# Decoder trunk on one core: held-back column sums, a rounded part taken from PSUM, and two first blocks by token half in layer 1

## The chip, the core and the metric

The kernel runs on one core of a Trainium2 chip. The core has TensorE (PE: matmuls and transposes), VectorE (DVE), ScalarE (ACT), GpSimd (POOL) and SyncE (SP), which here issues the loads. Each engine works its own instructions in the order in which the program lists them and waits at an instruction until the semaphores that it names have come. Matmuls write to PSUM, which has eight banks; VectorE and ScalarE carry results from there to SBUF. The metric is the time of one execution on the device in microseconds (us).

## The reference

A two-layer decoder trunk on 256 tokens of width 2048, all in float32. Per layer, with `mod` a row of 6 x 2048 values that depends on the vector `c` alone:

```python
mod = cond @ w_ada[l] + b_ada[l]
shift1, scale1, gate1, shift2, scale2, gate2 = split(mod, 6)
h = rms_norm(x, norm1_w[l]) * (1.0 + scale1) + shift1
mixed = mixer_groups(h, ..., w_in[l], ...)      # four head groups: GLA, retention, sliding window, HGRN2
x = x + gate1 * (mixed @ w_out[l])
h = rms_norm(x, norm2_w[l]) * (1.0 + scale2) + shift2
g_ff, u_ff = split(h @ w_ffn_in[l], 2)
x = x + gate2 * ((silu(g_ff) * u_ff) @ w_ffn_down[l])
```

After both layers comes a last `rms_norm`.

## The kernel before

**Matmuls.** Float32 products are made from three passes of a rounded format. An operand `raw` is split into a rounded part `hi` and a rest `lo = raw - hi`, and a product is `hi*hi + hi*lo + lo*hi`: three matmuls. A weight block is 512 rows by 512 columns. It comes as two *pieces* of 256 rows, 512 KB each. `prepare()` makes one piece: a load into `raw` on SP's queue (nine buffers), ScalarE rounds it (`whi`, line 243), VectorE subtracts (`wlo`, line 246). There are four buffers each of `whi` and `wlo`. `plan` is the list of blocks in the order in which they are used. `fill(n)` prepares pieces until n of them stand ready, and wherever `fill` is called, ScalarE and VectorE get the two splits at that place of their queues.

**Blocks.** `block()` (lines 339 to 341) takes both halves of the 256 tokens for each row tile. `blocks_by_token()` (lines 355 to 357) takes one or two whole blocks for the first 128 tokens (t = 0) and then for the other 128 (t = 1): 12 matmuls for each block and half, six for each piece. It first takes all its pieces, then runs, and after a named place (t, block, row tile) it calls what its table `after` has for it.

**Changes of stage.** Three times the whole residual `x` is needed at once: from the mixer of layer 0 to its FFN (A, near 547 us in the profile), from the FFN of layer 0 to layer 1 (B, near 1299 us), and from the mixer to the FFN of layer 1 (C, near 1756 us). At each, `last_blocks()` runs the last two blocks by token half and, as a half ends, does `add_x` (VectorE: `tmp` = product times gate, `x` = x + tmp; ScalarE: a square with its sum, called `junk`), and then `norm_first`: VectorE adds the four sums (`rstd`), ScalarE takes a root, VectorE inverts it and scales the first 512 columns (`xs`). `norm_steps()` then makes the next activations: TensorE transposes `xs` into a PSUM tile `m`, ScalarE applies scale `a` and shift `s` of each column (four instructions of 128 x 128 into `h`), VectorE rounds `h` (`hTh`) and subtracts (`hTl`). The first group of 512 columns (c = 0) is made by token half, groups 1 to 3 for all tokens at once. The first blocks of the next stage run by token half too, so that t = 0 can start while t = 1 is still being normalised.

**Column sums.** `s` and `a` come from `mod`. `ada()` adds up `cond[k] * w_ada[k]` on VectorE in the background (line 403, paced by `pump()` with due times `dl`), and `reduce_` (line 432) sums the 128 partitions of the result with eight matmuls of one column. `later` holds the reductions for a few blocks and then lets them go; `require(key)` forces one.

Of the kernel before, what the change touches and what calls it, by code (L numbers as in the profile page):

```python
# [11 lines left out]
F32 = mybir.dt.float32  # L12
# [68 lines left out]
def decoder(ctx: ExitStack, tc: tile.TileContext, x_d, c_d, pos_d, w_ada, b_ada, n1_d, w_in, w2_d, b2_d,  # L81
# [196 lines left out]
    done = set()  # L278

    def require(*key):  # L280
        while key not in done:
            if later:
                later.pop(0)[2]()
            else:
                bg.popleft()[1]()
# [131 lines left out]
    def ada_pair(l, which, g, dl, defer=6):  # L417
        base = 0 if which == 1 else 6144
        sv, av = colv[l, "s%d" % which], colv[l, "a%d" % which]
        r = ROWS["n1" if which == 1 else "n2"] + 16 * l  # L420

        def fin(acc):
            if defer:
                later.append([3, ("c", l, which, g), lambda: reduce_(acc)])
            else:
                reduce_(acc)

        def reduce_(a):
            ps = MB([P, 2, 4])
# [64 lines left out]
    def norm_steps(av, sv, his, los, xs, by_token=True):  # L494
        if by_token:
# [4 lines left out]
            for t in range(NT):  # L500
# [4 lines left out]
                for k in range(4):  # L505
                    A.activation(h[:, k], ps[:, k], AF.Identity, scale=av[:, k:k + 1], bias=sv[:, k:k + 1])
                split(h, hi[:, :, t * P:(t + 1) * P], lo[:, :, t * P:(t + 1) * P])
# [510 lines left out]
    for l in range(L):  # L1018
# [4 lines left out]
        else:  # L1023
            for g in range(4):
                for c0 in HG:
                    plan_block(w_in[l], g * 512, c0, 512)
            for c0, w in FIRST[3:]:
                for g in range(4):
# [45 lines left out]
    def hgrn(act, nsteps, l):  # L1074
# [5 lines left out]
        ev_q, ev_f, ev_k = tail_hg(l, pq, pf, qT, Pf, kT)  # L1080
        for g in range(4):
# [5 lines left out]
            if g < 3:  # L1087
                require("c", l, 1, g + 1)
                next(nsteps)
# [14 lines left out]
        chunk(act, W, 5904, 512, pg)  # L1104
        gs = T4([P, NT, 512], n="hg")
        gate_evac(pg, gs, l, 1, 0, 512)
# [126 lines left out]
    def last_blocks(bs, adds, key, nsteps, xs):  # L1233
        def added(t, b):
# [9 lines left out]
            if b == len(bs) - 1:  # L1244
# [3 lines left out]
                else:  # L1248
                    if t:
                        fill()  # L1250
                    xs.append(norm_first(t))

        after = {(t, b): lambda t=t, b=b: added(t, b) for t in range(NT) for b in range(len(bs))}
        if nsteps is not None:
            def first():
                next(nsteps)
                fill()
            after[1, 1, 1] = first
# [11 lines left out]
    for l in range(L):  # L1270
# [50 lines left out]
        for f0, npc in PIECES:  # L1321
            ah, al = [], []
            for c in range(f0, f0 + npc):
# [10 lines left out]
                if c == 0:  # L1334
                    def next_group(l=l):
                        require("c", l, 2, 1)
                        next(nsteps)
# [91 lines left out]
```

## Time and profile before

| | us |
|---|---|
| median of three runs (2508.48 to 2510.01) | 2508.67 |
| the profiled execution's own time | 2509.56 |
| its span, first to last instruction | 2507.8 |
| PE busy | 2408.2 (96%) |
| DVE busy | 1803.0 (72%) |
| ACT busy | 1100.7 (44%) |

The row of PE busy is the one to read first: TensorE is the engine that works nearly all the time, and the other engines and the loads have room. The mean granted clock of TensorE is 0.99. Busy shares are means over stages; what a change at a stage's end is worth has to be read there.

### The profile page before, as it was taken

What the parts mean: (1) busy time and instruction counts of PE and PEld (TensorE: products, weight loads), DVE (VectorE), ACT (ScalarE), POOL (GpSimd) and SP (SyncE); (2) the same over time, 40 slices, a digit from 0 to 9 for tenths busy, and PEclk for the clock granted to TensorE, in tenths of its full rate; (3) what the DMA queues carried; (4) which work ended last, traced back from release to release, by engine and by line L of the source; (5) the groups of instructions that cost most, each with busy time, mean ns of one, the idle gap of its engine ahead of it and who ended that gap; (6) DMA issues with size and microseconds to landing.
All of it is one profiled execution on the core that took longest, in us unless ns stands there. A gap on an engine that the chain in (4) does not pass through costs nothing. (4 is left out here: it accounts for less than half of the span.)

```text
span 2507.8 us, 32376 instructions
## 1 busy us (share of the span) xinstructions
PE 2408.2 (96%) x12030; PEld 2034.0 (81%) x12030; DVE 1803.0 (72%) x2032; ACT 1100.7 (44%) x1476; POOL 133.9 (5%) x143
## 2 busy tenths in 40 slices
PE   3998899999999999999989999999999999999998
PEld 3887778778888888888879998887788888888886
DVE  7898899877777667777767787866777555455456
ACT  3434434444443344344444444554544444443444
POOL 1001221000000000000000122100000000000000
PEclk9999999999999999999999999999999999999999
DMA  9997679968888888788767776666688565555563
GB/s 324 359 338 278 211 242 318 320 235 284 296 283 289 280 271 280 273 274 291 266 213 254 234 227 208 219 225 245 229 288 288 189 194 187 181 199 193 191 202 109
DMA packets 314910, 626.17 MB, mean 250 GB/s; under 512 B 21236, under 2 KB 34400, under 8 KB 314496
## 3 DMA queue, kind: packets, MB, share of 16 engines
q1 hardware_dynamic: 312800, 622.68, 73.4%
q8 instruction: 94, 1.54, 0.2%
q10 hardware_dynamic: 528, 1.14, 0.1%
q0 software_dynamic: 1424, 0.29, 0.1%
q14 instruction: 64, 0.52, 0.1%
HBM read 621.93 MB, written 2.10 MB: 249 GB/s over the span
## 5 line engine op out<-in xcount | busy, mean ns | idle before, releaser
L246 DVE TENSOR_TENSOR wlo<-raw,whi 128x1024 fp32r<-128x1024 f32 (+2 forms) x816 | 970.7, 1197 | 547.9 <-ACT whi L243 526.8
L243 ACT ACTIVATE whi<-raw 128x1024 fp32r<-128x1024 f32 (+2 forms) x816 | 836.5, 1034 | 877.0 <-PE d L341 710.3
L339 PE MATMUL d<-whi,hTh 128*128 128x512 f32 (+2 forms) x1888 | 734.7, 389 | 0.7 <-ACT whi L243 0.6
L340 PE MATMUL d<-wlo,hTh 128*128 128x512 f32 (+2 forms) x1888 | 723.1, 383 | 1.0 <-DVE wlo L246 1.0
L341 PE MATMUL d<-whi,hTl 128*128 128x512 f32 (+2 forms) x1888 | 723.8, 383 | 0.0
L403 DVE SCALAR_TENSOR_TENSOR acc<-raw,cond,acc 128x1024 f32<-128x1024 f32 x384 | 500.5, 1304 | 13.1 <-POOL acc L393 7.3
L341 PEld LDWEIGHTS d<-whi,hTl 128*128 128x128 f32 x1888 | 355.3, 188 | 70.4
L340 PEld LDWEIGHTS d<-wlo,hTh 128*128 128x128 f32 x1888 | 355.9, 189 | 67.9 <-DVE wlo L246 1.6
L339 PEld LDWEIGHTS d<-whi,hTh 128*128 128x128 f32 x1888 | 356.0, 189 | 67.4 <-ACT whi L243 1.3
L339 PE MATMUL d<-whi,ah 128*128 128x512 f32 x672 | 262.7, 391 | 0.0
L341 PE MATMUL d<-whi,al 128*128 128x512 f32 x672 | 261.7, 389 | 0.0
L340 PE MATMUL d<-wlo,ah 128*128 128x512 f32 x672 | 261.5, 389 | 0.0
L341 PEld LDWEIGHTS d<-whi,al 128*128 128x128 f32 x672 | 126.2, 188 | 26.5
L340 PEld LDWEIGHTS d<-wlo,ah 128*128 128x128 f32 x672 | 126.2, 188 | 25.9
L339 PEld LDWEIGHTS d<-whi,ah 128*128 128x128 f32 x672 | 126.2, 188 | 25.7
L376 PE MATMUL d<-hTh,whi 128*128 128x256 f32 x320 | 93.1, 291 | 4.6 <-DVE hTh L245 4.6
L339 PE MATMUL d<-whi,mh 128*128 128x512 f32 x224 | 89.5, 400 | 3.8 <-DVE tmp L999 3.4
L378 PE MATMUL d<-hTl,whi 128*128 128x256 f32 x320 | 92.4, 289 | 0.7 <-DVE hTl L246 0.7
L377 PE MATMUL d<-hTh,wlo 128*128 128x256 f32 x320 | 92.0, 288 | 0.0
L340 PE MATMUL d<-wlo,mh 128*128 128x512 f32 x224 | 88.2, 394 | 2.5 <-DVE wlo L246 2.5
L341 PE MATMUL d<-whi,ml 128*128 128x512 f32 x224 | 87.8, 392 | 0.0
L339 PE MATMUL m<-whi,hTh 128*128 128x512 f32 (+2 forms) x184 | 68.5, 372 | 6.3 <-DVE hg L1127 4.7
(286 smaller groups left out, 2161.0 us busy)
## 6 DMA issues: line engine op xcount, KB each, us to landing
raw<-in_w_ada_dram SPq DMA_DIRECT2D x384, 512.0 KB, 5.3
raw<-in_w_ffn_in_dram SPq DMA_DIRECT2D x352, 512.0 KB, 4.7
raw<-in_w_in_dram SPq DMA_DIRECT2D x176, 512.0 KB, 5.3
raw<-in_w_ffn_down_dram SPq DMA_DIRECT2D x176, 512.0 KB, 4.8
raw<-in_w_out_dram SPq DMA_DIRECT2D x64, 512.0 KB, 5.3
raw<-in_w_in_dram SPq DMA_DIRECT2D x32, 256.0 KB, 3.3
raw<-in_w_in_dram SPq DMA_DIRECT2D x16, 272.0 KB, 3.7
x<-in_x_dram SPq DMA_DIRECT2D x2, 1024.0 KB, 9.1
```

The costliest lines, as they stand in the source:

```text
L243: A.activation(hi, src, AF.Copy)
L246: V.tensor_tensor(out=lo, in0=src, in1=hi.bitcast(F32), op=ALU.subtract)
L339: TE.matmul(o, xh, wh[:, kk], start=st, stop=False)
L340: TE.matmul(o, xh, wl[:, kk], start=False, stop=False)
L341: TE.matmul(o, xl, wh[:, kk], start=False, stop=sp)
L376: TE.matmul(o, a, hi4[:, k], start=st and f % 2 == 0, stop=False, skip_group_check=True)
L377: TE.matmul(o, b, hi4[:, k], start=False, stop=False, skip_group_check=True)
L378: TE.matmul(o, a, lo4[:, k], start=False, stop=sp and f % 2 == 1, skip_group_check=True)
L403: V.scalar_tensor_tensor(out=st["a"], in0=raw, scalar=cond[:, k:k + 1], in1=st["a"], op0=ALU.mult, op1=ALU.add)
```

## The change

There are four edits.

1. *Held-back sums.* Some `reduce_` calls are no longer let go by `later`. They are put into `parked`, and `fill_pe()` runs the oldest of them at a named place: one behind the last blocks of the old stage, one ahead of the transposes of t = 1, and at B one more behind the first blocks of t = 0. Two are held back at A, three at B and two at C. The due times of all sums change.
2. *The rounded part from PSUM.* For c = 0, ScalarE writes `hTh` straight from the transposes, and VectorE makes the unrounded `h` from the same PSUM tile itself (lines 519, `TENSOR_SCALAR`) and subtracts (line 521), in two pairs.
3. *Where pieces are prepared.* At the end of the last t = 1, `fill()` is no longer called two row tiles before the end; `fill(2)` stands behind `add_x` and ahead of `norm_first`, and `fill()` behind it. In the first blocks of the FFN the transposes of t = 1 stand one row tile later.
4. *Layer 1 by two blocks.* The first blocks by token half are now columns 5392 and 5904 (before 5392 alone). The part of column block 5904 for the first 512 rows is copied out to SBUF and added on VectorE when the other three row groups are done.

```diff
+    def fill_pe(n=1):
+        for key in list(parked)[:n]:
+            parked.pop(key)()
+
     def require(*key):
         while key not in done:
-            if later:
+            if key in parked:
+                parked.pop(key)()
+            elif later:
                 later.pop(0)[2]()
...
         def fin(acc):
-            if defer:
+            if park:
+                parked["c", l, which, g] = lambda: reduce_(acc)
+            elif defer:
...
                 h = T2([P, 4, P], n="h")
                 for k in range(4):
-                    A.activation(h[:, k], ps[:, k], AF.Identity, scale=av[:, k:k + 1], bias=sv[:, k:k + 1])
-                split(h, hi[:, :, t * P:(t + 1) * P], lo[:, :, t * P:(t + 1) * P])
+                    A.activation(hi[:, k, t * P:(t + 1) * P], ps[:, k], AF.Identity, scale=av[:, k:k + 1],
+                                 bias=sv[:, k:k + 1])
+                for k2 in range(2):
+                    for k in (2 * k2, 2 * k2 + 1):
+                        V.tensor_scalar(out=h[:, k], in0=ps[:, k], scalar1=av[:, k:k + 1], scalar2=sv[:, k:k + 1],
+                                        op0=ALU.mult, op1=ALU.add)
+                    V.tensor_tensor(out=lo[:, 2 * k2:2 * k2 + 2, t * P:(t + 1) * P], in0=h[:, 2 * k2:2 * k2 + 2],
+                                    in1=hi[:, 2 * k2:2 * k2 + 2, t * P:(t + 1) * P].bitcast(F32), op=ALU.subtract)
                 yield
...
-                for c0 in HG:
+                for c0 in (HG[0], 5904) + HG[1:] if g == 0 else HG:
...
-                blocks_by_token([(act[0][0], act[1][0], W, 0, 5392, 512, pv, True, False)],
-                                {(0, 0): lambda: next(nsteps), (1, 0): fill})
...
+                blocks_by_token([(act[0][0], act[1][0], W, 0, 5392, 512, pv, True, False),
+                                 (act[0][0], act[1][0], W, 0, 5904, 512, pf, True, True)],
+                                {(0, 1, 1): next_token, (0, 1): next_group, (1, 0): lambda: fill(2), (1, 1): fill})
+                for t in range(NT):
+                    urgent.append(lambda t=t: A.activation(gs[:, t], pf[t], AF.Copy))
...
-        chunk(act, W, 5904, 512, pg)
...
+        for g in range(1, 4):
+            block(act[0][g], act[1][g], W, g * 512, 5904, 512, pg, g == 1, g == 3)
+        flush_urgent()
+
+        def rest(t):
+            V.tensor_tensor(out=gs[:, t], in0=pg[t], in1=gs[:, t], op=ALU.add)
+            A.activation(gs[:, t], gs[:, t], AF.Silu)
...
-                ada_pair(l, 1, g, at(w_in[l], max(g - 1, 0) * 512, 5392) - (12 if g else 14))
+                ada_pair(l, 1, g, at(w_in[l], 0, 5392) - (10, 8, 6, 4)[g], 3, g in (1, 2, 3))
...
-            ada_pair(l, 2, g, at(w_fi[l], max(g - 1, 0) * 512, 0) - (16 if g else 14))
+            ada_pair(l, 2, g, at(w_fi[l], 0, 0) - (13, 9, 6, 0)[g], 3, g in (1, 2))
...
                     if t:
+                        fill(2)
+                        fill_pe()
+                    xs.append(norm_first(t))
+                    if t:
                         fill()
-                    xs.append(norm_first(t))
...
-            def first():
-                next(nsteps)
-                fill()
-            after[1, 1, 1] = first
+            after[1, 1, 1] = lambda: next(nsteps)
...
                     def next_group(l=l):
                         require("c", l, 2, 1)
+                        fill_pe()
                         next(nsteps)
 
+                    def next_token():
+                        fill_pe()
+                        next(nsteps)
+
...
-                                    {(0, 1, 0): lambda: next(nsteps), (0, 1): next_group, (1, 0): lambda: fill(2), (1, 1): fill})
+                                    {(0, 1, 1): next_token, (0, 1): next_group, (1, 0): lambda: fill(2), (1, 1): fill})
```

How the queues change is shown at A; B and C have the same pattern (the numbers behind names are buffers of this build). ScalarE before, from the root of t = 0 (line 481) on; `whi_4819` and `whi_4825` are the second and third piece of the FFN's first two blocks:

```order
L481 ACTIVATE rstd_4770<-rstd_4770,eps 128x1
L243 ACTIVATE whi_4790<-raw_4788 128x1024
L506 ACTIVATE h_4810<-m_4805,s_0_121,a_0_122 128x128 x4
L243 ACTIVATE whi_4819<-raw_4817 128x1024
L243 ACTIVATE whi_4825<-raw_4823 128x1024
L474 ACTIVATE junk_4835,ssq<-x_91 128x512
L474 ACTIVATE junk_4840,ssq<-x_91 128x512
L481 ACTIVATE rstd_4842<-rstd_4842,eps 128x1
L243 ACTIVATE whi_4854<-raw_4852 128x1024
```

and now, where `whi_4793` and `whi_4816` are the second and third piece:

```order
L490 ACTIVATE rstd_4727<-rstd_4727,eps 128x1
L243 ACTIVATE whi_4747<-raw_4745 128x1024
L515 ACTIVATE hTh_4760<-m_4762,s_0_121,a_0_122 128x128 x4
L483 ACTIVATE junk_4784,ssq<-x_91 128x512
L483 ACTIVATE junk_4789,ssq<-x_91 128x512
L243 ACTIVATE whi_4793<-raw_4791 128x1024
L490 ACTIVATE rstd_4808<-rstd_4808,eps 128x1
L243 ACTIVATE whi_4816<-raw_4814 128x1024
L243 ACTIVATE whi_4826<-raw_4824 128x1024
```

The second piece has moved from ahead of both squares (`junk`) to behind them, and the third from there to behind the root of t = 1. VectorE at the same place now, with what each row waits for: the first row is the `x` of column group 2, the last the second piece's subtraction.

```order
L1015 TENSOR_TENSOR x_91<-x_91,tmp_4751 128x512 [waits DVE_49]
L519 TENSOR_SCALAR h_4767<-m_4762,a_0_122,s_0_121 128x128 [waits Activation_49]
L519 TENSOR_SCALAR h_4767<-m_4762,a_0_122,s_0_121 128x128
L521 TENSOR_TENSOR hTl_4761<-h_4767,hTh_4760 128x2x128 [waits DVE_49]
L519 TENSOR_SCALAR h_4767<-m_4762,a_0_122,s_0_121 128x128 x2
L521 TENSOR_TENSOR hTl_4761<-h_4767,hTh_4760 128x2x128 [waits DVE_49]
L1014 TENSOR_TENSOR tmp_4786<-d_4556,gate_3294 128x512 [waits PE_49]
L1015 TENSOR_TENSOR x_91<-x_91,tmp_4786 128x512 [waits DVE_49]
L246 TENSOR_TENSOR wlo_4794<-raw_4791,whi_4793 128x1024 [waits DMAHW3_49,Activation_49]
```

Before, these rows stood here:

```order
L1000 TENSOR_TENSOR x_91<-x_91,tmp_4794 128x512
L245 CAST hTh_4803<-h_4810 128x4x128
L246 TENSOR_TENSOR hTl_4804<-h_4810,hTh_4803 128x4x128
L246 TENSOR_TENSOR wlo_4820<-raw_4817,whi_4819 128x1024
L246 TENSOR_TENSOR wlo_4826<-raw_4823,whi_4825 128x1024
L999 TENSOR_TENSOR tmp_4837<-d_4605,gate_3129 128x512
L1000 TENSOR_TENSOR x_91<-x_91,tmp_4837 128x512
```

Two instructions on the activations have become six, and the second and third piece's subtractions have left the place ahead of the last `tmp` and `x`. The semaphore in the first `TENSOR_SCALAR` is that of the last of the four ScalarE instructions above it. TensorE now, from the end of `w_out` on: a held-back sum, then six matmuls on the first piece, then the second piece.

```order
L364 MATMUL d_4556<-whi_4689,ml_3968 128x512
L441 MATMUL m_4797<-ones,acc_3529 128x1 x8
L362 MATMUL d_4820<-whi_4747,hTh_4760 128x512
L363 MATMUL d_4820<-wlo_4748,hTh_4760 128x512
L364 MATMUL d_4820<-whi_4747,hTl_4761 128x512
L362 MATMUL d_4820<-whi_4747,hTh_4760 128x512
L363 MATMUL d_4820<-wlo_4748,hTh_4760 128x512
L364 MATMUL d_4820<-whi_4747,hTl_4761 128x512
L362 MATMUL d_4820<-whi_4793,hTh_4760 128x512
L363 MATMUL d_4820<-wlo_4794,hTh_4760 128x512
```

Six matmuls on the second piece and six on the third follow, and then the second sum and the transposes of t = 1, ahead of the fourth piece. Before, there was no sum, and the transposes stood three matmuls earlier, behind 15 matmuls in place of 18.

## Rows read from the trace of the kernel before

**Rows 1.** The page's first part: busy us (share of the span) xinstructions.
```profile
PE 2408.2 (96%) x12030; PEld 2034.0 (81%) x12030; DVE 1803.0 (72%) x2032; ACT 1100.7 (44%) x1476; POOL 133.9 (5%) x143
```

**Rows 2.** Timeline at A: start us, us, instruction, [idle before, releaser].
```profile
545.40 0.60 PE L503 MATMUL m<-identt,xs 128*128 128x128 f32 x4
546.03 1.51 ACT L506 ACTIVATE h<-m,s,a 128x128 f32<-128x128 f32 x4 [0.88 <-PE m L503]
546.99 0.40 PE L357 MATMUL d<-whi,ml 128*128 128x512 f32 x1
547.05 0.69 DVE L1000 TENSOR_TENSOR x<-x,tmp 128x512 f32<-128x512 f32 x1
548.74 0.50 PE L355 MATMUL d<-whi,hTh 128*128 128x512 f32 x1 [1.35 <-DVE hTh L245]
...
551.60 0.68 DVE L999 TENSOR_TENSOR tmp<-d,gate 128x512 f32<-128x512 f32 x1
552.31 0.69 DVE L1000 TENSOR_TENSOR x<-x,tmp 128x512 f32<-128x512 f32 x1
553.85 0.16 DVE L480 TENSOR_REDUCE rstd<-ssq 128x1 f32<-128x4 f32 x1 [0.85 <-ACT junk L474]
554.24 1.04 ACT L243 ACTIVATE whi<-raw 128x1024 fp32r<-128x1024 f32 x1
554.57 0.48 DVE L487 TENSOR_SCALAR xs<-x,rstd 128x512 f32<-128x512 f32 x1
555.20 0.63 PE L503 MATMUL m<-identt,xs 128*128 128x128 f32 x4 [2.49 <-DVE xs L487]
558.48 1.67 DVE L487 TENSOR_SCALAR xs<-x,rstd 128x512 f32<-128x512 f32 x4
...
560.39 0.48 PE L355 MATMUL d<-whi,hTh 128*128 128x512 f32 x1
```

**Rows 3.** Timeline of PE at C.
```profile
1756.12 0.40 PE L357 MATMUL d<-whi,ml 128*128 128x512 f32 x1
...
1768.79 0.48 PE L355 MATMUL d<-whi,hTh 128*128 128x512 f32 x1
```

**Rows 4.** Timeline of PE at B.
```profile
1298.70 0.40 PE L357 MATMUL d<-whi,al 128*128 128x512 f32 x1
...
1309.05 0.77 PE L355 MATMUL m<-whi,hTh 128*128 128x512 f32 x1 [2.21 <-DVE hTh L245]
...
1315.94 0.36 PE L376 MATMUL d<-hTh,whi 128*128 128x256 f32 x1
```

**Rows 5.** Timeline of DVE and ACT ahead of B: a split behind a square.
```profile
1282.36 0.69 DVE L1000 TENSOR_TENSOR x<-x,tmp 128x512 f32<-128x512 f32 x1
1283.72 1.05 ACT L243 ACTIVATE whi<-raw 128x1024 fp32r<-128x1024 f32 x1
1284.80 1.23 DVE L246 TENSOR_TENSOR wlo<-raw,whi 128x1024 fp32r<-128x1024 f32 x1 [1.74 <-ACT whi L243]
```

**Rows 6.** Timeline of PE at a column sum that is not held back.
```profile
1778.00 1.84 PE L432 MATMUL m<-ones,acc 128*128 128x1 f32 x16
1779.70 0.49 PE L339 MATMUL d<-whi,hTh 128*128 128x512 f32 x1
```

**Rows 7.** Groups of DVE by form: xcount | busy us, mean ns | idle before.
```profile
L553 DVE SCALAR_TENSOR_TENSOR y<-o,s,hg 128x128 f32<-128x128 f32 x16 | 4.5, 345 | 0.1
L655 DVE TENSOR_TENSOR gs<-gs 128x256 f32<-128x256 f32 x14 | 6.0, 427 | 0.2 <-POOL gs L654 0.2
L212 DVE TENSOR_SCALAR kk<-ang 128x128 f32<-128x128 f32 x1 | 0.2, 227 | 0.0
```

**Rows 8.** Three stretches of PE: us, busy (matmuls), granted clock, DMA share, GB/s.
```profile
549.80:552.55 2.75, 2.75 (x13) 1.00 0.35 80
555.20:560.40 5.20, 5.19 (x22) 0.67 0.36 118
1309.05:1314.30 5.25, 5.25 (x12) 0.50 0.32 100
```

More of the change, by code (lines that the diff above doesn't have):

```diff
@@ L278, in decoder @@
     done = set()
+    parked = {}
+    def fill_pe(n=1):
+        for key in list(parked)[:n]:
+            parked.pop(key)()
     def require(*key):
         while key not in done:
-            if later:
+            if key in parked:
+                parked.pop(key)()
+            elif later:
                 later.pop(0)[2]()
@@ L415, in ada, with ada_pair @@
             bg.append((dl, lambda k=k: unit(k)))
-    def ada_pair(l, which, g, dl, defer=6):
+    def ada_pair(l, which, g, dl, defer=6, park=False):
         base = 0 if which == 1 else 6144
@@ L1024, in decoder @@
             for g in range(4):
-                for c0 in HG:
+                for c0 in (HG[0], 5904) + HG[1:] if g == 0 else HG:
                     plan_block(w_in[l], g * 512, c0, 512)
             for c0, w in FIRST[3:]:
-                for g in range(4):
+                for g in range(1 if c0 == 5904 else 0, 4):
                     plan_block(w_in[l], g * 512, c0, w)
@@ L1080, in hgrn, with next_group @@
         ev_q, ev_f, ev_k = tail_hg(l, pq, pf, qT, Pf, kT)
+        gs = T4([P, NT, 512], n="hg")
+        def next_token():
+            fill_pe()
+            next(nsteps)
+        def next_group():
+            require("c", l, 1, 1)
+            fill_pe()
+            next(nsteps)
         for g in range(4):
@@ L1083, in hgrn @@
                 block(act[0][g], act[1][g], W, g * 512, 5392, 512, pv, False, g == 3)
-            else:
-                blocks_by_token([(act[0][0], act[1][0], W, 0, 5392, 512, pv, True, False)],
-                                {(0, 0): lambda: next(nsteps), (1, 0): fill})
-            if g < 3:
-                require("c", l, 1, g + 1)
-                next(nsteps)
+                if g < 3:
+                    require("c", l, 1, g + 1)
+                    next(nsteps)
+            else:
+                blocks_by_token([(act[0][0], act[1][0], W, 0, 5392, 512, pv, True, False),
[3 more added lines that the diff above has]
+                    urgent.append(lambda t=t: A.activation(gs[:, t], pf[t], AF.Copy))
             hi, lo = act[0][g], act[1][g]
@@ L1103, in hgrn @@
         pg = [DB() for _ in range(NT)]
-        chunk(act, W, 5904, 512, pg)
-        gs = T4([P, NT, 512], n="hg")
-        gate_evac(pg, gs, l, 1, 0, 512)
+        for g in range(1, 4):
[4 more added lines that the diff above has]
+            A.activation(gs[:, t], gs[:, t], AF.Silu)
+            g3 = gs[:, t].rearrange("p (h d) -> p h d", d=P)
+            G.tensor_tensor(out=g3, in0=g3, in1=nwb[:, l, 1, :].unsqueeze(1).to_broadcast([P, 4, P]), op=ALU.mult)
+        for t in range(NT):
+            urgent.append(lambda t=t: rest(t))
         mt = mixed_tiles()
@@ L1249, in added @@
                     if t:
+                        fill(2)
+                        fill_pe()
+                    xs.append(norm_first(t))
+                    if t:
                         fill()
-                    xs.append(norm_first(t))
         after = {(t, b): lambda t=t, b=b: added(t, b) for t in range(NT) for b in range(len(bs))}
         if nsteps is not None:
-            def first():
-                next(nsteps)
-                fill()
-            after[1, 1, 1] = first
+            after[1, 1, 1] = lambda: next(nsteps)
         blocks_by_token(bs, after)
@@ L1336, in next_group, with next_token @@
                         require("c", l, 2, 1)
+                        fill_pe()
+                        next(nsteps)
+                    def next_token():
+                        fill_pe()
                         next(nsteps)
                     blocks_by_token([(his[0], los[0], w_fi[l], 0, b, 512, ps, True, False) for b, ps in ((0, pg), (DFF, pu))],
-                                    {(0, 1, 0): lambda: next(nsteps), (0, 1): next_group, (1, 0): lambda: fill(2), (1, 1): fill})
+                                    {(0, 1, 1): next_token, (0, 1): next_group, (1, 0): lambda: fill(2), (1, 1): fill})
                     for g in range(1, 4):
```

## Prediction, made before the changed kernel ran

> **What bounds the kernel now.** The page's first part comes first [rows 1]: the reader should see that TensorE works 96% of the span, so that nothing done faster elsewhere counts unless TensorE waits for it. It waits at the three changes of stage, and the timeline at A shows how [rows 2]. The last matmul of `w_out` starts at 546.99 and TensorE stands 1.35 us for `hTh`; it runs 15 matmuls and stands 2.49 us for `xs` of t = 1, because `x` of the last column group ends only at 553.00; the first matmul of t = 1 starts at 560.39. C goes from 1756.12 to 1768.79 [rows 3]; B from 1298.70 to `block_T` at 1315.94 [rows 4]. From end to start that is 13.4, 12.7 and 17.2 us. Last the windows [rows 8]: 549.80 to 552.55 ran at a granted clock of 1.00 (2.4 GHz), one matmul each 0.23 us (twelve steps and part of one more); behind the 2.49 us wait the clock is 0.67, a mean of the two levels; and at B twelve matmuls behind the 2.21 us wait [rows 4] ran at 0.50 (1.2 GHz) in 5.25 us where 12 x 0.23 = 2.75 would do. So a wait here costs its own time and then half speed for a while. The order of the matmuls away from the changes is the same but for the moved sums, so the sum is made over A, B and C.
>
> **The sums.** A column sum in the busy stretch costs 1.70 us, from 1778.00 to the next matmul at 1779.70 [rows 6]. Seven leave such stretches: 7 x 1.70 = 11.9 us saved. What each costs at its new place comes out of the walk below.
>
> **A, walked by the new order.** TensorE: the first sum runs 547.22 to 548.92, under the old wait for `hTh`. Two matmuls later it wants `hTl`. ScalarE's four instructions end at 547.54, `x` of group 2 at 547.74 [rows 2], and then VectorE has four `TENSOR_SCALAR` and two subtractions in place of a cast and a subtraction. No row of before is a 128 x 128 instruction of VectorE from PSUM. The nearest [rows 7] are `L553`, 345 ns for one and 16 in 4.5 us (0.28 apart), and from SBUF `L212`, 227 ns; a subtraction of 256 columns is `L655`, 427 ns. I take four at 0.28 and two at 0.43, 2.0 us; low (227 ns, 0.16 apart) 1.55, high (345 ns end to end) 2.23. `hTl` is there at 549.75, in time, and the six matmuls on the first piece end at about 550.3. This far the change is ahead.
>
> Now the second piece. Its rounding stands behind both squares of t = 1, so behind `x` of the last group. VectorE does `tmp` and `x` in 0.68 + 0.69 and a little [rows 2], 549.75 + 1.40 = 551.15. What comes behind an `x` is shown ahead of B [rows 5]: `x` ends at 1283.05, `whi` behind it at 1284.77 (+1.72), `wlo` at 1286.03 (+2.98). So `whi` is there at 552.87 and `wlo` at 554.13. TensorE stands 2.6 us, runs one matmul, stands 1.0, and runs the other five by 555.3.
>
> The third piece's rounding is behind the root of t = 1. The sum of the four squares (`L480`) is behind that `wlo` and two small copies of 0.16 us (priced as the `L480` row), so it starts at 554.45; `xs` starts 0.72 later and `whi` of the third piece 0.39 later [rows 2], ending 555.88, its `wlo` at 557.1. TensorE stands 0.6 and 1.0 and ends the piece at 558.25. Then the second sum, 1.70, with nothing to hide under, since `xs` has stood ready since 555.65: to 559.95. Then the transposes of t = 1: from their start to the end of ScalarE's four is 2.14 (545.40 to 547.54), VectorE's six then take 2.1, and from `xs` of group 1 to the first matmul of t = 1 is 1.91 (558.48 to 560.39) [rows 2]: 566.1. Meanwhile TensorE has only the six matmuls of the fourth piece (before it had nine) and stands about 2.8 us.
>
> At A that is 566.1 - 560.39 = 5.7 later, less two sums of 1.70: **+2.3**. C is A moved by 1209.13 (the two last matmuls of `w_out`): 1775.2 for 1768.79, +6.4 - 3.4 = **+3.0**. At B, moved by 751.71, the sum of group 1 runs inside the last wait and adds two small copies, 0.3: t = 1 starts at 1318.1 and, with two blocks, `block_T` 24 x 0.23 = 5.5 later, 1323.6. Before, `block_T` came at 1315.94, but the first 512 rows of column block 5904 (5.5) and three sums (5.1) still had to be run: 1326.5. **-2.9**. Together **+2.4**; the bounds of VectorE's six, taken twice at each change, make it -0.3 to +3.8.
>
> **The clock.** The walk has all new matmuls at full clock, and there are about 8.0 us of waits at A (2.6, 1.0, 0.6, 1.0, 2.8) where there were 3.84 [rows 2], in short runs of five or six matmuls between them. What half clock costs is bounded below by nothing, if the sums keep the clock up, and above by the runs of t = 0, the transposes' sum and the twelve matmuls after all doubled: 1.0 + 1.7 + 2.5 = 5.2 per change. Between them stand A, where the stretch at 0.67 lost 5.2 x 0.33 = 1.7, and B, where twelve matmuls lost 2.5 [rows 8]. I take 2.0 for each change, **+6.0** (0 to 15.6).
>
> **What is costed at nothing.** Edit 4's two copies out of PSUM, two adds and `Silu` from SBUF (0.4 to 0.7 us each, by `L655` and `L1000`) lie on ScalarE and VectorE, busy 44% and 72% [rows 1], while TensorE has full blocks to run; if a PSUM tile came free late it would be 0.5 us once. The moved `fill` changes when loads are issued; the DMA share is 0.32 to 0.36 in these stretches [rows 8], so I see no late piece. If one were late, what is late next is that piece's rounding, and the piece's own wait grows.
>
> **Two rules of the Trainium skill.** In the new order VectorE's first `TENSOR_SCALAR` waits for the last of ScalarE's four, since both read one PSUM tile; no row of before has the two there. The Trainium skill, "PSUM — Partial Sum Buffer", section "PSUM bank collisions raise a hardware error", says that two engines must be kept apart in a bank even when both only read. By it the two cannot run side by side, which speaks against edit 2: if they could, each change would be about 1.5 us shorter, 4.5 in all. No row of before bears on it.
>
> For the price of those instructions, the same skill's "VectorE: DVE Perf Modes", section "Why PSUM operands drop a tier", has float32 from PSUM at the lowest rate. That speaks for 345 ns; by 227 ns the sum would be 2.7 us less. Rows of before decide only between the bounds.
>
> **Sum and time.** 2.4 + 6.0 = 8.4. The profiled execution took 2509.56 (span 2507.8 and 1.8 around it), so 2518.0; the median of the runs is 0.89 below that execution, so **2517**. By the bounds of VectorE and clock prices of 1.0 to 3.5 per change, this case reaches from 2512 to 2523.
>
> **Rivals.**
> - *The clock falls no further than before.* For it: the sums fill 1.7 us of each old wait, and behind the 1.35 us wait at A the clock was back at 1.00 [rows 8]. Against: more waits than before. It gives the walk alone, +2.4: 2511.
> - *The splits do not hold TensorE (faster).* If the second piece's `wlo` is there by 550.3 and the third's by 551.7, TensorE runs its 18 matmuls through, and waits only for `xs` of t = 1. t = 1 then starts at 560.9 at A; with the sums that is -2.9, at C -2.2 and at B -8.1, -13.2 in all: 2495.5. It decides at `x` of the last group: that would have to end by 550.3 - 2.98 = 547.3. With nothing but `tmp` and `x` left for VectorE after 547.74 it ends at 549.15, 1.8 us too late. Only a piece rounded earlier than I read the order, or `tmp` long ahead, would bring it.
> - *Low clock all through the changes.* For it: B's twelve at 0.50 behind a wait of only 2.21. Price 6 per change instead of 2, with transposes and copies late as well: +18, 2526.5.
> - *The change does nothing.* The old waits for `hTh` and `xs` go and the new ones for pieces are as long: within a microsecond or two of 2509.
>
> **Chances.** 0.2% of this time is 5.0 us, about what a measurement can tell from no change. The forecast has 0.57, the steady clock 0.18, the faster rival 0.12, low clock 0.11, nothing 0.02. Faster takes the second rival and a little of the first, 0.13. Same takes the rest of the first, the last, and the low edge of the forecast (2512 to 2513.7), 0.21. Slower is 0.66. The range from 2507 to 2526 holds the forecast, the steady clock and half of low clock; it leaves out the fast rival and the upper half of low clock, some 0.2.
>
> **What the new profile would show.** Right: in the FFN's first blocks at A and C, TensorE's waits on `whi` (2.6 and 0.6 us) and `wlo` (1.0 twice); about 2.8 us ahead of group 1's transposes, put down to `xs`; no long wait ahead of the transposes of t = 1; `TENSOR_SCALAR` from PSUM at about 345 ns; seven sums inside the changes; t = 1 starting some 19 us behind the last matmul of `w_out`; a granted clock below 1 there. Wrong: `whi` of the second piece before 550.3 would make the splits harmless and the change faster; a clock of 1.00 would leave the walk alone; a wait on a load would mean that the moved `fill` cost what I put at nothing.

## The result, and the profile after

The changed kernel takes 2549.79 us (median of four runs, 2545.26 to 2550.70); the kernel before 2508.78. The ratio is 1.0157 (95% interval 1.0145 to 1.0169): slower by about 40 us. The forecast was slower, but by 8. The two profiled executions, 2549.55 and 2509.56, are 40.0 apart and are compared from here on.

The page's first part of the changed kernel answers to [rows 1].

```profile
PE 2426.9 (95%) x12030; PEld 2049.9 (80%) x12030; DVE 1802.3 (71%) x2058; ACT 1101.7 (43%) x1478; POOL 132.3 (5%) x143
```

The instructions of TensorE are the same in number, and VectorE does no more work; so the 40 us are waits of TensorE and a lower clock, and the question is where. Both kernels run the same matmuls on weight pieces in nearly the same order, so one can take the start of the n-th of them in each trace and subtract. That gives this table (us; each figure is the difference of two starts in one trace, and the last column the difference to the kernel before; a "block" is here the work of 12 matmuls of 512 columns, and two of 256 columns count as one):

| stretch, in blocks | before | after | |
|---|---|---|---|
| start, 0 to 64 | 242.5 | 241.5 | -1.0 |
| first mixer, 64 to 112 | 194.0 | 212.6 | **+18.6** |
| `w_out` of layer 0, 112 to 128 | 52.2 | 49.9 | -2.2 |
| A and what is around it, 128 to 144 | 55.4 | 68.7 | **+13.3** |
| FFN of layer 0, 144 to 392 | 695.3 | 689.8 | -5.5 |
| B, 392 to 424 | 106.3 | 108.3 | +2.0 |
| second mixer, 424 to 496 | 266.5 | 269.3 | +2.9 |
| `w_out` of layer 1, 496 to 528 | 97.9 | 98.7 | +0.8 |
| C, 528 to 544 | 53.4 | 64.6 | **+11.2** |
| the rest, from 544 | 687.1 | 687.0 | 0.0 |

The FFN's -5.5 are the three sums that left it. A and C are longer, as forecast, but by more. And the largest single piece, the first mixer, lies where the change edits nothing but the due times of the background.

The timeline of TensorE at A in the changed kernel answers to [rows 2]; the number in brackets is the idle time before the instruction and what ended it.

```profile
562.30 0.40 PE L364 MATMUL d<-whi,ml 128*128 128x512 f32 x1
562.53 1.84 PE L441 MATMUL m<-ones,acc 128*128 128x1 f32 x16
564.24 0.48 PE L362 MATMUL d<-whi,hTh 128*128 128x512 f32 x1
...
568.39 0.59 PE L362 MATMUL d<-whi,hTh 128*128 128x512 f32 x1 [2.53 <-ACT whi L243]
569.65 0.79 PE L363 MATMUL d<-wlo,hTh 128*128 128x512 f32 x1 [0.67 <-DVE wlo L246]
570.24 0.63 PE L364 MATMUL d<-whi,hTl 128*128 128x512 f32 x1
...
574.69 3.41 PE L441 MATMUL m<-ones,acc 128*128 128x1 f32 x16
577.96 1.09 PE L512 MATMUL m<-identt,xs 128*128 128x128 f32 x4
...
583.37 1.38 PE L534 MATMUL m<-identt,xs 128*128 128x128 f32 x8 [1.76 <-DVE xs L496]
584.51 0.48 PE L362 MATMUL d<-whi,hTh 128*128 128x512 f32 x1
```

The reader should see the walk of the prediction: six matmuls, 2.53 us for the second piece's `whi`, 0.67 for its `wlo`, no wait ahead of the transposes of t = 1, and 1.76 us ahead of group 1's. And one thing more: from the second piece on a matmul takes 0.63 us where it took 0.39, and the second sum 3.41 us in place of 1.84.

Windows of TensorE in the changed kernel (us, busy (matmuls), granted clock, DMA share, GB/s): the first mixer, A, the part of B with its waits, and C.

```profile
288.62:501.24 212.62, 195.02 (x1023) 0.95 0.75 250
564.24:584.51 20.27, 15.24 (x55) 0.66 0.25 85
1323.00:1339.00 16.00, 10.77 (x62) 1.00 0.34 110
1786.09:1807.04 20.95, 15.90 (x55) 0.61 0.25 82
```

The same stretch of the first mixer before:

```profile
289.69:483.70 194.01, 187.25 (x1035) 0.99 0.84 282
```

TensorE was idle there for 6.8 us (194.01 - 187.25) and is now for 17.6 (212.62 - 195.02); the other 7.8 us are matmuls that run longer, at 0.95 in place of 0.99.

Of TensorE's waits there VectorE ends 11.8 us of 17.3 (before, 4.9 of 6.6), and neither TensorE nor VectorE nor ScalarE waits for a weight load. What stops TensorE is seen well near 330 us, in the timeline of the changed kernel (GpSimd, VectorE, TensorE).

```profile
327.75 1.82 POOL L669 TENSOR_TENSOR gs<-gs 128x256 f32<-128x256 f32 x1 [1.33 <-DVE kd L654]
329.51 0.96 POOL L400 MEMSET acc<- 128x1024 f32 x1
330.76 1.03 POOL L402 DMA_DIRECT2D acc<-in_b_ada_dram  x2 [0.29 <-POOL acc L400]
...
329.90 0.46 DVE L670 TENSOR_TENSOR gs<-gs 128x256 f32<-128x256 f32 x1
333.73 1.28 DVE L410 SCALAR_TENSOR_TENSOR acc<-raw,cond,acc 128x1024 f32<-128x1024 f32 x1 [3.37 <-DMA acc<-in_b_ada_dram]
334.93 0.42 DVE L637 TENSOR_TENSOR qd<-gqk,gs 128x256 f32<-128x256 f32 x1
335.26 0.98 DVE L654 TENSOR_TENSOR kd<-gqk,gs 64x128 f32<-64x128 f32 x4
...
335.68 2.64 PE L663 MATMUL m<-qd,kd 128*128 128x64 f32 x15 [3.44 <-DVE kd L654]
```

A new column sum begins here. GpSimd clears its buffer and loads the bias into it, but both stand behind the mixer's `gs` on GpSimd's queue. VectorE's first instruction of that sum stands among the mixer's own, waits 3.37 us for the load, and `qd` and `kd` are queued behind it; TensorE waits 3.44 us for `kd`. Of VectorE's waits in this mixer (us in total, times, longest) the load makes 10.2 us, in two places:

```profile
DVE wlo L246 <- ACT whi L243: 20.2, 12, 3.8
DVE acc L410 <- DMA acc<-in_b_ada_dram: 10.2, 2, 6.9
```

In the kernel before the load makes none there, and the largest entry is

```profile
DVE wlo L246 <- ACT whi L243: 11.5, 9, 3.8
```

Order alone can do the same, with nothing to wait for. At the mixer's start VectorE works two units of a column sum (a unit is one row block of `w_ada`) ahead of `y`, though the root that `y` needs was done at 287.0, and TensorE waits 2.50 us:

```profile
288.78 2.60 DVE L410 SCALAR_TENSOR_TENSOR acc<-raw,cond,acc 128x1024 f32<-128x1024 f32 x2
291.50 1.13 DVE L568 SCALAR_TENSOR_TENSOR y<-o,s,hg 128x128 f32<-128x128 f32 x4
292.00 1.16 PE L555 MATMUL m<-identt,y 128*128 128x128 f32 x4 [2.50 <-DVE y L568]
```

In the kernel before VectorE stands ready at this place 0.86 us ahead of the root, and TensorE never waits for `y` in this mixer.

A is longer by more than its walk for the same reason of pace: the table has 13.3, the walk below 8.8. Behind it the background stands in a lump ahead of two pieces:

```profile
595.71 5.25 DVE L410 SCALAR_TENSOR_TENSOR acc<-raw,cond,acc 128x1024 f32<-128x1024 f32 x4
600.88 2.35 DVE L246 TENSOR_TENSOR wlo<-raw,whi 128x1024 fp32r<-128x1024 f32 x2
...
602.15 0.50 PE L347 MATMUL d<-wlo,hTh 128*128 128x512 f32 x1 [2.60 <-DVE wlo L246]
602.49 0.40 PE L348 MATMUL d<-whi,hTl 128*128 128x512 f32 x1
602.72 0.56 PE L346 MATMUL d<-whi,hTh 128*128 128x512 f32 x1
603.08 0.63 PE L347 MATMUL d<-wlo,hTh 128*128 128x512 f32 x1
```

Four units of a column sum, 5.25 us, keep VectorE from a `wlo`; TensorE waits 2.60 us and then runs at 0.63 a matmul again.

### The profile page after: what moved, and what is told of

It reads as the page before. It is cut to its first block, busy times and chain, and to the rows that moved or that the text cites. A ratio compares the mean times of both kernels' runs of the same rounds, so it can differ in the third digit from the quotient of the medians.

```text
span 2547.8 us, 32391 instructions
## 1 busy us (share of the span) xinstructions
PE 2426.9 (95%) x12030; PEld 2049.9 (80%) x12030; DVE 1802.3 (71%) x2058; ACT 1101.7 (43%) x1478; POOL 132.3 (5%) x143
## 5 line engine op out<-in xcount | busy, mean ns | idle before, releaser
L410 DVE SCALAR_TENSOR_TENSOR acc<-raw,cond,acc 128x1024 f32<-128x1024 f32 x384 | 492.4, 1282 | 32.8 <-DMA acc<-in_b_ada_dram 21.3
L348 PEld LDWEIGHTS d<-whi,al 128*128 128x128 f32 x672 | 126.1, 188 | 26.4
```

The costliest lines, as they stand in the source:

```text
L348: TE.matmul(o, xl, wh[:, kk], start=False, stop=sp)
L410: V.scalar_tensor_tensor(out=st["a"], in0=raw, scalar=cond[:, k:k + 1], in1=st["a"], op0=ALU.mult, op1=ALU.add)
```

## The experiments

**Theory 1:** there are two causes. The due times of the column sums, which only looked like bookkeeping, put VectorE's background at worse places (some 23 us, in the mixers and behind A); and the pieces prepared late hold TensorE at the changes of stage, with the clock falling behind. **Rival:** the due times are harmless, and the moved sums, splits and buffers disturb the mixers too. Later rivals stand with their runs. Medians are compared with runs of the kernel before on the same chip: 2510.03 us for `e1` to `e4`, 2509.94 for `e5` to `e8`, 2509.59 for `e9` to `e11` and 2509.33 for `e12`.

**The due times alone** (`e1_dues_only`), in the kernel before. They are those of twelve column sums, four ahead of layer 1 and four ahead of each FFN; the sums of the gates keep theirs.

```diff
-                ada_pair(l, 1, g, at(w_in[l], max(g - 1, 0) * 512, 5392) - (12 if g else 14))
+                ada_pair(l, 1, g, at(w_in[l], 0, 5392) - (10, 8, 6, 4)[g])
-            ada_pair(l, 2, g, at(w_fi[l], max(g - 1, 0) * 512, 0) - (16 if g else 14))
+            ada_pair(l, 2, g, at(w_fi[l], 0, 0) - (13, 9, 6, 0)[g])
```

> The kernel before with nothing but the changed kernel's due times for the column sums. Theory 1 (the due times shift VectorE's background instructions in the mixers, where VectorE is nearly full, and that cost 18.6 us in the first mixer and 4.7 in the second): no gain and no loss at the three changes of stage, so 2509 + 23 = about 2532 us (2522 to 2540). Rival (the moved sums, pieces and buffers disturb the mixers, and the due times by themselves are harmless): 2509, within 5 us.

Measured: 2530.78, ratio 1.0083 (1.0070 to 1.0097), slower by 20.8. By the table's stretches of its profiled execution: first mixer +17.4, A +4.3, B -0.3, C -0.3. The rival falls: numbers that name no instruction cost half of the whole loss. The A row shows that the lump behind A is the due times' as well. The second mixer's +2.9 is not theirs alone (0.0 here).

**The change without its due times** (`e2_old_dues`): the same two lines in the changed kernel set back.

```diff
-                ada_pair(l, 1, g, at(w_in[l], 0, 5392) - (10, 8, 6, 4)[g], 3, g in (1, 2, 3))
+                ada_pair(l, 1, g, at(w_in[l], max(g - 1, 0) * 512, 5392) - (12 if g else 14), 3, g in (1, 2, 3))
-            ada_pair(l, 2, g, at(w_fi[l], 0, 0) - (13, 9, 6, 0)[g], 3, g in (1, 2))
+            ada_pair(l, 2, g, at(w_fi[l], max(g - 1, 0) * 512, 0) - (16 if g else 14), 3, g in (1, 2))
```

> The changed kernel with all four edits, but with the due times of the kernel before. Theory 1: the 23 us of the mixers come back, 2550 - 23 = about 2527 us (2519 to 2532), and the changes of stage keep their loss (A 13, C 12, B 2 us longer, sums included). Rival: 2550, within 5 us.

Measured: 2524.43 (2519.62 to 2532.45), ratio 1.0062 (1.0043 to 1.0081). The first mixer is at 191.9 us, even 2.1 below before; A stays +8.6, C +6.7, and B is +7.9. The median is 14.4 above before. This kernel's runs lie 13 us apart, and its profile shows why they may: at B nearly the same wait for the second piece (first line) as in the changed kernel (second line) was followed by low clock for twenty microseconds (third line), where the changed kernel ran at 1.00.

```profile
1303.95 0.49 PE L362 MATMUL m<-whi,hTh 128*128 128x512 f32 x1 [2.45 <-ACT whi L243]
1327.09 0.49 PE L362 MATMUL m<-whi,hTh 128*128 128x512 f32 x1 [2.42 <-ACT whi L243]
1304.50:1325.00 20.50, 18.98 (x66) 0.50 0.25 78
```

**Edit 2 alone** (`e3_psum_only`): in the kernel before, the four ScalarE instructions write `hi`, and VectorE's six replace `split`, as in the diff of the change.

```diff
-                    A.activation(h[:, k], ps[:, k], AF.Identity, scale=av[:, k:k + 1], bias=sv[:, k:k + 1])
-                split(h, hi[:, :, t * P:(t + 1) * P], lo[:, :, t * P:(t + 1) * P])
+                    A.activation(hi[:, k, t * P:(t + 1) * P], ps[:, k], AF.Identity, scale=av[:, k:k + 1],
+                                 bias=sv[:, k:k + 1])
...
+                        V.tensor_scalar(out=h[:, k], in0=ps[:, k], scalar1=av[:, k:k + 1], scalar2=sv[:, k:k + 1],
+                                        op0=ALU.mult, op1=ALU.add)
```

> The kernel before with nothing but the rounded part from PSUM (edit 2). Theory 1: at each change the x of the last column group comes about 0.9 us later (six instructions of 2.0 us on VectorE in place of two of 1.1), so the wait for xs grows by as much, and t = 1 is later by 0.9 too; three times 1 to 2 us, 2511 to 2514. Rival (the rounded part is ready earlier, by VectorE's cast of 0.4 us, and the waits for it of 1.35 and 0.75 us shrink): 2506 to 2509.

Measured: 2515.27, ratio 1.0021 (1.0012 to 1.0031), slower by 5.2, a little more than theory 1 had; A +1.9, B +0.9, C +3.4. In its timeline at A `x` of the last group ends 8.15 us behind the start of the transposes (545.80 to 553.26 + 0.69) where it was 7.60 (545.40 to 553.00, [rows 2]), and later on group 1's transposes wait for `xs`, as they did not before:

```profile
548.07 0.72 DVE L510 TENSOR_SCALAR h<-m,a,s 128x128 f32<-128x128 f32 x2
548.83 0.42 DVE L512 TENSOR_TENSOR hTl<-h,hTh 128x256 fp32r<-128x256 f32 x1
549.17 0.72 DVE L510 TENSOR_SCALAR h<-m,a,s 128x128 f32<-128x128 f32 x2
549.93 0.42 DVE L512 TENSOR_TENSOR hTl<-h,hTh 128x256 fp32r<-128x256 f32 x1
...
553.26 0.69 DVE L1006 TENSOR_TENSOR x<-x,tmp 128x512 f32<-128x512 f32 x1
...
561.66 0.64 PE L525 MATMUL m<-identt,xs 128*128 128x128 f32 x2 [1.31 <-DVE xs L487]
```

**The change with old due times and old places of the pieces** (`e4_old_dues_old_fill`): as `e2_old_dues`, and

```diff
                     if t:
-                        fill(2)
                         fill_pe()
-                    xs.append(norm_first(t))
-                    if t:
                         fill()
+                    xs.append(norm_first(t))
...
-            after[1, 1, 1] = lambda: next(nsteps)
+            def first():
+                next(nsteps)
+                fill()
+            after[1, 1, 1] = first
```

> The changed kernel with the due times of the kernel before and, at the end of the last t = 1, the pieces prepared where they were before (fill two row tiles before the end, and ahead of norm_first). Theory 1 (the late pieces cause the waits of 2.5 and 0.7 us behind the first six matmuls at A and C and, through them, the fall to 1.2 GHz): 2527 less about 16 us, 2505 to 2513. Rival (the clock falls there because the column sums stand in the stretch): it stays at 2520 to 2530.

Measured: 2503.21, ratio 0.9974 (0.9964 to 0.9984): faster than before, and below theory 1's range. The rival falls: with the same sums at A and the pieces early, the stretch from the first FFN matmul to t = 1 takes 12.89 us in place of 20.27, at full clock.

```profile
545.89:558.78 12.89, 9.68 (x54) 1.00 0.45 140
1748.35:1761.26 12.91, 9.69 (x54) 1.00 0.43 140
```

The second line is the same stretch at C. What waits are left at A are 0.35 and 0.54 us for a `wlo` and 2.11 ahead of group 1. Late pieces cost 21.2 us by the medians (2524.43 - 2503.21).

**The same without edit 2** (`e5_no_psum`): `split(h, ...)` back in its place.

> As e4_old_dues_old_fill (due times and places of the pieces as before, held-back sums and two first blocks in layer 1), and without edit 2: the rounded part is made by VectorE from h again. Theory 1 (VectorE's six instructions make x of the last group late and so t = 1, as in e3_psum_only, which cost 5.2 us at three changes): 2503 - 5 = 2498 us (2495 to 2500). Rival (with a sum ahead of the first blocks the early rounded part pays, and edit 2 costs nothing here): 2503, within 2 us.

Measured: 2503.72 (2497.53 to 2507.83), ratio 0.9969 (0.9958 to 0.9981). The median is the rival's, the spread covers both. By stretch, A is 2.0 and C 1.6 shorter than in `e4_old_dues_old_fill`, and B 3.1 longer, with clock lost at B in this execution. Whether edit 2 costs anything among these edits is not settled.

**Held-back sums alone** (`e6_sums_only`): in the kernel before, `parked` and `fill_pe`, two sums at A and two at C.

```diff
-            ada_pair(l, 2, g, at(w_fi[l], max(g - 1, 0) * 512, 0) - (16 if g else 14))
+            ada_pair(l, 2, g, at(w_fi[l], max(g - 1, 0) * 512, 0) - (16 if g else 14), 3, g in (1, 2))
...
                     if t:
+                        fill_pe()
                         fill()
...
-                                    {(0, 1, 0): lambda: next(nsteps), (0, 1): next_group, (1, 0): lambda: fill(2), (1, 1): fill})
+                                    {(0, 1, 0): next_token, (0, 1): next_group, (1, 0): lambda: fill(2), (1, 1): fill})
```

> The kernel before with nothing but two held-back sums at A and two at C, at its own due times. Theory 1 (the sums run under waits that stand there anyway): four sums of 1.70 leave the busy stretches, -6.8, and A and C get no longer, or up to 2 us shorter by a steadier clock: 2510 - 7 to 2510 - 10, 2500 to 2503. Rival (the sums are on the path at their new place too, as the walk in the prediction had the second one): 2507 to 2511.

Measured: 2502.07, ratio 0.9968 (0.9957 to 0.9980). A is 0.7 and C 2.8 shorter with two more sums in each: with the pieces early, a sum in a wait costs nothing. So held-back sums by themselves are a gain.

**Only the due times of layer 0's FFN** (`e7_dues_layer0`), in the kernel before:

```diff
-            ada_pair(l, 2, g, at(w_fi[l], max(g - 1, 0) * 512, 0) - (16 if g else 14))
+            ada_pair(l, 2, g, at(w_fi[l], 0, 0) - (13, 9, 6, 0)[g] if l == 0 else at(w_fi[l], max(g - 1, 0) * 512, 0) - (16 if g else 14))
```

> The kernel before with the new due times for the four column sums of layer 0's FFN alone. Theory 1 (they set the pace of the background in the first mixer, and all of the +17 there and the +4 at A that e1_dues_only showed are theirs, and +2 to +4 of the second mixer's are not): 2510 + 20 = 2527 to 2533. Rival (the pace comes from the whole list, layer 1's due times too): 2510, within 4 us.

Measured: 2529.49, ratio 1.0080 (1.0064 to 1.0096); first mixer +15.9, A +2.3. Four numbers do it.

**The same due times without the bias load** (`e8_dues_no_bias`): as `e1_dues_only`, and

```diff
                 st["a"] = T4([P, np_, w], n="acc")
-                G.memset(st["a"], 0.0)
-                for j in range(np_):
-                    nc.gpsimd.dma_start(st["a"][0:1, j, :], b_ada[l:l + 1, c0 + j * D:c0 + j * D + w])
...
-            V.scalar_tensor_tensor(out=st["a"], in0=raw, scalar=cond[:, k:k + 1], in1=st["a"], op0=ALU.mult,
+            V.scalar_tensor_tensor(out=st["a"], in0=raw, scalar=cond[:, k:k + 1], in1=st["a"] if k else raw, op0=ALU.mult,
```

> As e1_dues_only, but each background sum starts from its first weight rows and not from a cleared buffer with the bias loaded into it, so VectorE never waits there for GpSimd and its load; the bias b_ada is left out of the sums and one row block is added unscaled. Theory 1a (the two waits of VectorE for that load, 10.3 us in the first mixer, make TensorE late by 4.8 us at 330 and by some 3 us at 410, and the clock falls behind): 2531 less 7 to 12, 2519 to 2524. Rival 1b (it is the order of the background instructions among the mixer's own on VectorE, whatever they wait for): 2527 to 2532.

Measured: 2519.58, ratio 1.0037 (1.0023 to 1.0051), 11.2 below `e1_dues_only`. In the first mixer +17.4 becomes +11.6, and the start of the kernel is 4.3 shorter. So the load makes about a third of the mixer's loss. Both theories hold a part: two thirds are left when nothing waits for it. Of that rest the trace shows the kind: TensorE's waits in the mixer are 13.0 us for 6.6 before, and 6.4 of them are for `y`, the one of 2.50 us above among them (2.49 here); the matmuls take 5.3 us longer, at a clock of 0.97 for 0.99.

**The control** (`e12_before_no_bias`): the same edit in the kernel before.

> The control for e8_dues_no_bias: the kernel before, with the bias b_ada left out of the background sums in the same way (each starts from its first weight rows). In the first mixer the kernel before has no wait of VectorE for the bias load. Theory 1a (the gain of e8 in the mixer was its two waits): no more than 2 us there, and some of the 4 us ahead of the mixer; 2505 to 2510. Rival (leaving out the clearing and the bias is worth as much in any order): 2498 to 2501.

Measured: 2507.55, ratio 0.9994 (0.9985 to 1.0003); first mixer +0.15, start -1.1. Leaving the bias out is worth nothing where VectorE doesn't wait for it, so what `e8_dues_no_bias` gained in the mixer was the wait.

**Due times the other way** (`e10_dues_earlier`): in the kernel before, layer 0's four FFN sums two blocks earlier.

```diff
-            ada_pair(l, 2, g, at(w_fi[l], max(g - 1, 0) * 512, 0) - (16 if g else 14))
+            ada_pair(l, 2, g, at(w_fi[l], max(g - 1, 0) * 512, 0) - (16 if g else 14) - (2 if l == 0 else 0))
```

> The kernel before with the due times of layer 0's four FFN column sums two blocks earlier, the other way from the change. Theory 1c (any change of the pace puts the background at other places among the first mixer's instructions on VectorE, and the order of before is a good one by luck or tuning): slower too, 2515 to 2530. Rival 1d (only later due times cost, because they leave more for the end of the mixer and for A): 2507 to 2512.

Measured: 2523.32, ratio 1.0057 (1.0043 to 1.0071). The start is 7.3 longer and the first mixer 4.7. So it is not that later is bad: either way costs. That it is VectorE's order here too is likely but was not followed in this trace.

**The change with only the places of the pieces set back** (`e11_new_dues_old_fill`): the second diff of `e4_old_dues_old_fill`, in the changed kernel.

> The changed kernel with the pieces prepared where they were before, and nothing else undone; the new due times stay. Theory 1 (the two causes, due times 25 us and piece places 21 us, add up and are all of it): 2550 - 21 = 2526 to 2531. Rival (with the pieces early the changes of stage take up what the mixers lose, or the due times bring other waits there): below 2520, or above 2535.

Measured: 2529.79, ratio 1.0085 (1.0070 to 1.0101); first mixer +18.1. From the changed kernel's 2549.79 the old due times take 25.4, the old places 20.0, both 46.6: the two causes add, 45.4 for 46.6, and what is left of the change is a gain.

**Best of each** (`e9_best_of_each`): due times and piece places of before, the sums of `e6_sums_only` at A and C, and layer 1's beginning of `e4_old_dues_old_fill`, with edit 2 at B alone.

```diff
+                if av is colv[1, "a1"]:
...
+                else:
...
-                                    {(0, 1, 1): next_token, (0, 1): next_group, (1, 0): lambda: fill(2), (1, 1): fill})
+                                    {(0, 1, 0): next_token, (0, 1): next_group, (1, 0): lambda: fill(2), (1, 1): fill})
```

> Due times and piece places as before; two held-back sums at A and C as in e6_sums_only, and the beginning of layer 1 as in e4_old_dues_old_fill (two blocks, three held-back sums, rounded part from PSUM, at B alone). Theory 1 (what the single runs gave at their places adds up): 2502.1 less 5.4 for the three sums that leave layer 0's FFN and less 3.6 at B: 2493 us (2490 to 2497). Rival (what is saved at a change is lost again to the clock, at the next wait): 2500 to 2504, as e4, e5 and e6.

Measured: 2498.37, ratio 0.9958 (0.9946 to 0.9970), 11.2 faster than before and the best of all. It lies between theory and rival: the three sums gave their 5.5, A and C are as in `e6_sums_only`, but B is only 0.5 shorter, where `e4_old_dues_old_fill` had 3.1. B ran at 0.84 here (first line), and at 1.00 there:

```profile
1290.00:1312.00 22.00, 20.33 (x105) 0.84 0.33 98
1291.90:1312.20 20.30, 18.59 (x110) 1.00 0.36 107
```

## Why the prediction was off

**The step that failed** is the sentence "The order of the matmuls away from the changes is the same but for the moved sums, so the sum is made over A, B and C." The order of TensorE's matmuls is nearly the same, but in the mixers TensorE also waits for VectorE, and VectorE's order had changed, since the due times pace the background through it. In the prediction they stand in no sum. [Rows 1] say that VectorE has 28% to spare, and that hid it: in the kernel before it is busy 176.9 us of the first mixer's 194.0 (91%), and in stretches it has next to nothing to spare (31.5 us of the 34 from 302 to 336, 58.1 of the 59 from 368 to 427). `e1_dues_only` gave 20.8 us for this term where the sum had none. With the due times set back the change costs 14.4 us (`e2_old_dues`), and that lies inside the stated range.

**The sums.** Right: 1.70 each saved where they left; the FFN of layer 0 with its three is 5.5 shorter.

**The walk.** From the last matmul of the old stage to the first of t = 1 (to `block_T` at B) the prediction with its clock term has 21.1 us at A, 26.9 at B and 21.1 at C (the walk's ends less [rows 2 to 4], plus 2.0 each). Measured are 22.2 (562.30 to 584.51), 26.4 (1321.08 to 1347.45) and 22.9 (1784.17 to 1807.04): 71.5 for 69.1. So the three changes of stage cost 10.8 where the forecast had 8.4. That they are so near is partly luck, as the next paragraph shows. Order and sizes of the waits at the second piece were right (2.42 to 2.53 us for `whi`, 0.67 to 0.77 for `wlo`). The waits at the third piece did not come but for 0.76 us for `wlo` at B, and that for `xs` of group 1 was 1.76 at A and C and 1.46 at B for 2.8.

**The clock** was mis-sized, and the missing waits paid for it. The same matmuls, sums and transposes that keep TensorE busy for 9.68 and 9.69 us at full clock (`e4_old_dues_old_fill`) took 15.24 at A and 15.90 at C in the changed kernel: 5.6 and 6.2 us lost, where the sum had 2.0 each. At B the stretch with the waits ran at 1.00, but behind the last of them the clock fell, and 8.22 x (1 - 0.79) = 1.7 us were lost there:

```profile
1339.23 1.59 PE L534 MATMUL m<-identt,xs 128*128 128x128 f32 x8 [1.46 <-DVE xs L496]
1339.23:1347.45 8.22, 8.21 (x33) 0.79 0.07 10
```

That is 13.5 for 6.0; the three changes came out only 2.4 longer than forecast, so the waits were some 5 us shorter. At A and C, with slow matmuls on the second piece, TensorE did not wait for the third piece's `wlo`; at B, with fast ones, it did, 0.76 us. A wait and a slow stretch behind it are not two terms to be added here.

**VectorE's six instructions.** Taken at 2.0 us, they took 2.2. The groups of the changed kernel:

```profile
L519 DVE TENSOR_SCALAR h<-m,a,s 128x128 f32<-128x128 f32 x24 | 8.7, 404 | 7.5 <-ACT hTh L515 7.5
L521 DVE TENSOR_TENSOR hTl<-h,hTh 128x256 fp32r<-128x256 f32 x12 | 5.1, 425 | 0.4
```

404 ns for one and 0.36 apart (8.7 / 24), dearer than the 345 ns at 0.28 of [rows 7], and far from `L212`'s 227. (The prediction says that no row of before is a 128 x 128 instruction of VectorE from PSUM; `L553` is one, since its `o` is written by matmuls.) The Trainium skill, "VectorE: DVE Perf Modes", section "Why PSUM operands drop a tier", has float32 from PSUM at the lowest rate; the trace agrees as far as it goes: 404 ns from PSUM, 227 for a `TENSOR_SCALAR` of that size from SBUF.

The first row shows VectorE waiting 7.5 us for ScalarE's `L515`: the two read one PSUM tile in turn. The Trainium skill, "PSUM — Partial Sum Buffer", section "PSUM bank collisions raise a hardware error", asks for that; no run here let them read at once. But this wait is not what edit 2 costs: the kernel before waited nearly as long at the same places, for `h` from the same engine (first line; the second is `e3_psum_only`).

```profile
DVE hTh L245 <- ACT h L506: 5.3, 4, 2.4
DVE h L510 <- ACT hTh L506: 6.1, 4, 2.4
```

What is new in `e3_psum_only` is the length of the six. At A VectorE goes to them straight from `x`, and they take 2.20 us (548.07 to 550.27) where the cast and the subtraction took 1.67. By that `x` of the last group is 0.55 later. The rest of its +1.9 at A comes behind: the transposes of t = 1 take 1.09 us for 0.63, and group 1's wait 1.31 for `xs`.

**What was costed at nothing.** The copies, adds and `Silu` of edit 4 show no wait of TensorE's. The second mixer's +2.9 is 0.0 with the due times alone (`e1_dues_only`) and +1.0 with them set back (`e2_old_dues`): it takes the due times and other edits together. One wait of TensorE, for ScalarE's `kd`, is more than all of it. It was 1.24 us before and 1.27 in `e1_dues_only`, is 2.46 in `e2_old_dues` and 5.41 in the changed kernel, and what stands ahead of it is a bias load again: VectorE waits for it, so its `gs` is late, then ScalarE's, then `kd`.

```profile
1551.37 1.28 DVE L410 SCALAR_TENSOR_TENSOR acc<-raw,cond,acc 128x1024 f32<-128x1024 f32 x1 [2.88 <-DMA acc<-in_b_ada_dram]
1553.81 0.63 ACT L769 ACTIVATE gs<-gs 128x512 f32<-128x512 f32 x1 [4.37 <-DVE gs L768]
1555.53 1.86 PE L615 MATMUL m<-gqk,kd 128*128 128x128 f32 x7 [5.41 <-ACT kd L607]
```

None of the waits at A shown above was for a load of weights. A load did cost, but on GpSimd's queue and in the mixers.

**The rivals.** "The splits do not hold TensorE" was excluded rightly for this kernel, and it is what `e4_old_dues_old_fill` made of it. "Low clock all through the changes" is what A and C show, at its price of 6 (5.6 and 6.2), but not B. Its sum is short: 3 x 6 and the walk's 2.4 are 20.4, not 18.

**Still open.** Of the 17.4 us that the due times cost in the first mixer, 5.8 are the bias load (`e8_dues_no_bias` against `e1_dues_only`). The other 11.6 are 6.4 more of TensorE's waits, as much as it waits for `y`, and 5.3 of matmuls at a lower clock. That VectorE's order makes them is read from the trace and was not tried apart. What keeps the clock up at B in one execution and lets it fall in another, behind nearly the same wait, is open as well.

## What to carry to other kernels

A number that only paces background work is an edit to every engine that the work runs on: compare the order on the fullest of those engines all along the program, not only where the change was made, and read its busy share by stage. When a wait is to be filled, first ask what stands behind it: the sums were free at A only when the pieces behind them were ready, and the two places where these are prepared (21 us) decided between loss and gain. Try the parts of a bundle apart: here the held-back sums gained 8 us, and two other parts hid it.

## What was not expected of the hardware

With no more VectorE work (1796.0 us busy for 1803.0 in all), a stage in which VectorE is busy 91% of the time became 17.4 us longer when nothing but due times moved (`e1_dues_only`), and moving the same four due times either way cost 13.7 (earlier) or 19.6 us (later; `e10_dues_earlier`, `e7_dues_layer0`). And the granted clock is not a function of the wait: in the changed kernel's B it stayed at 1.00 for 12 us behind a wait of 2.42 us, and fell behind the next long one, of 1.46.
